# A hybrid RWKV-7 and attention layer: x, w_o blocks and early up products around the first norm, issued in another order

## The chip, the cores and the metric

The kernel runs on one core of one Trainium2 chip. The metric is the device time of one execution in microseconds (us); the number that is compared is the median of several executions. All times below are of this kernel on this one core. TensorE runs at 1.2 or 2.4 GHz; the profile gives the granted clock of a stretch as a share of the higher level, so that 0.50 is the lower one.

## What is computed

One step of a single layer for 512 new frames (`x_prompt`) and 128 further frames of running streams (`x_sample`), 2048 columns wide, all in float32. Half of the columns go through an RWKV-7 recurrence, half through an attention with forget gates; both meet in `w_o`, and a norm and an MLP with another norm follow. The change concerns the lines from `w_o` to `w_up`:

```python
    mix = jnp.concatenate([y_r, y_f], axis=-1) @ w_o
    h = layer_norm(ALPHA * x + mix, ln1_g, ln1_b)
    ffn = jnp.square(jax.nn.relu(h @ w_up)) @ w_down
    out = layer_norm(ALPHA * h + ffn, ln2_g, ln2_b)
```

## The kernel before

**Tiles.** The 640 frames are five token tiles (t = 0 to 3 from `x_prompt`, t = 4 from `x_sample`) of 128 rows. Every float32 product is made of three TensorE matmuls on a high and a low part of each side (`three`). A raw tile is split into them by two instructions: ScalarE copies it to the high part, and VectorE subtracts that from the raw tile for the low part.

**w_o.** The 2048 output columns are four groups n of 512. For groups 1 and 2 a loop takes eight steps s; each loads a block of 256 rows of `w_o` (`rawo{n}_{s}`, 0.52 MB), splits it (`hio`, `loo`) and adds 5 x 2 x 3 = 30 matmuls into five PSUM banks `po{n}_{t}` (`tokens`). `OB = (1, 4, 4)` gives raw blocks one buffer, high and low parts four each. When a group ends, `add_x` fetches a piece of x (`xz`, 128 x 512, 0.26 MB) for each token tile, adds it to the bank (into `acc[t]`) and takes its statistics, and the bank is free for the next group. `xz` has two buffers, and the first holder of one is `gbr`, the norm's gain and offset, read later by a transpose. The adds of group 0 (whose products stand earlier) run in the middle of group 1. Group 3 is done for each token tile apart (`last_columns`), with the tile's norm and its store to `hscr[t]`.

**The up products.** The MLP's first product is a Strassen-like scheme on halves of 320 tokens and 1024 rows: the normed tile h, transposed, gives blocks `11` and `21` (made by `first_tokens`: transposes on TensorE, gain and offset and high part on ScalarE, low part on VectorE) and `22`, `t1` to `t4` (made by `sums(k)`, k = 0 to 7: four groups of transposes into banks b12, b22, b11, b21, then about a dozen vector steps). A loop over pairs of column blocks (`pair(i)`, seven products of 24 matmuls each) uses them all; the raw weights of a pair, `rw`, are loaded by `load_w` into the tiles that held `acc`. To have TensorE at work while the sums are made, the products of the first four pairs with `11` and `21` are taken ahead: `early(i, j)`, 24 matmuls each into a bank `pe{i}`, j = 0 with block `11`, j = 1 with `21`. Their weights are two quarters (`we`), each loaded, split (`hie`, `loe`) and used. After j = 0 ScalarE copies the bank to `xe`, after j = 1 it applies the ReLU.

**Buffers.** The tag `s` of the pool `stgu` is a ring of four: raw tiles of `first_tokens`, the raw quarters of the early weights, and two tiles for each call of `sums` (`t0_k`, `t1_k` in the trace: b12s and t1, t2 and b22s) take their turn in it. High parts of early weights have three buffers, low parts two. PSUM is split in five banks `pq` and three `pd`.

**Order.** TensorE's order is that of the program text (`manual_schedule` for that engine); the orders of VectorE, ScalarE, GpSimd and of SyncE, which issues the loads and stores, are set by the scheduler of the framework. An engine works its instructions off in order: one that waits holds all behind it, on SyncE too.

Of the kernel before, what the change touches and what calls it, by code (L numbers as in the profile page):

```python
# [11 lines left out]
F32 = mybir.dt.float32  # L12
F32R = mybir.dt.float32r
BF16 = mybir.dt.bfloat16
AF = mybir.ActivationFunctionType
# [4 lines left out]
P = 128  # L20
# [149 lines left out]
def hybrid_layer_kernel(  # L170
# [1001 lines left out]

    lst = [lnp.tile([P, 4, 6], F32, name=f"lst{t}", bufs=1) for t in range(NTT)]

    def add_x(n, t, pt):

        a = acc[t][:, n * 512:(n + 1) * 512]
        xz = lnp.tile([P, 512], F32, tag="xz", name=f"xz{n}{t}", bufs=2)
        SY.dma_start(xz, xrows(t)[:, n * 512:(n + 1) * 512])
        V.scalar_tensor_tensor(out=a, in0=xz, scalar=ALPHA, in1=pt, op0=ALU.mult, op1=ALU.add)  # L1180
        V.bn_stats(out=lst[t][:, n, :], in_=a)

# [19 lines left out]
    for n in range(1, 3):  # L1202
        pts = [bank(f"po{n}_{t}") for t in range(NTT)]
        for s in range(8):
            tokens(w_o, s * 256, 2, n * 512, yT.hi, yT.lo, 2 * s, pts,
                   s == 0, s == 7, f"o{n}_{s}", b=OB)
            if n == 1 and s == 4:
                for t in range(NTT):
                    add_x(0, t, acc[t][:, 0:512])
        for t in range(NTT):  # L1210
            add_x(n, t, pts[t])
# [3 lines left out]

    pts = [bank(f"po3_{t}") for t in range(NTT)]
    for s in range(4):
        tokens(w_o, s * 256, 2, 1536, yT.hi, yT.lo, 2 * s, pts, s == 0, False, f"o3_{s}", b=OB)
    ends = [split([w_o[s * 256:s * 256 + 256, 1536:2048].rearrange("(k p) f -> p k f", p=P)], [P, 2, 512], f"o3_{s}", OB)
            for s in range(4, 8)]  # L1220

    def last_columns(t):
        for s, (hi, lo) in enumerate(ends):
# [56 lines left out]
    def early_weights(i, j):  # L1280

        ws = []
        for q in range(2):
            w = quarter(f"we{i}{j}{q}")
            r0 = (8 * j + 4 * q) * P
            SY.dma_start(w, w_up[r0:r0 + 4 * P, 2 * i * P:2 * i * P + P].rearrange("(k p) f -> p k f", p=P))
            ws.append(parts_w(w, f"e{i}{j}{q}"))
        return ws

    for t in range(4):  # L1290
        last_columns(t)
    parts("11", ((c11p, "c11h"), (c11p, "c11l")))
    first_tokens("11", 0, range(KH))
    first_weights = early_weights(0, 0)
    last_columns(4)
    ln.close()

# [14 lines left out]
    def sums(k):  # L1312


        b12 = turn_h(bank(f"b12_{k}"), k, True)
        b22 = turn_h(bank(f"b22_{k}"), KH + k, True)
        b11 = turn_h(bank(f"b11_{k}"), k, False)
        b21 = turn_h(bank(f"b21_{k}"), KH + k, False)
        two = [stgu.tile([P, 2, HF], F32, tag="s", name=f"t{n}_{k}", bufs=4) for n in range(2)]
        b12s, t1, t2, b22s = two[0][:, 0, :], two[0][:, 1, :], two[1][:, 0, :], two[1][:, 1, :]  # L1320
        t3, t4 = b22s, b12s

        def out(b, raw, shift=None):
            oh, ol = (x[:, k, :] for x in H[b])
            if shift is None:
                A.activation(oh, raw, AF.Copy)
                V.tensor_tensor(out=ol, in0=raw, in1=oh.bitcast(F32), op=ALU.subtract)
            else:
                A.activation(oh, raw, AF.Identity, bias=shift)
                V.scalar_tensor_tensor(out=ol, in0=raw, scalar=shift, in1=oh.bitcast(F32), op0=ALU.add, op1=ALU.subtract)  # L1330

        A.activation(b12s, b12, AF.Copy, scale=gain(k))
        A.activation(b22s, b22, AF.Copy, scale=gain(KH + k))
        V.scalar_tensor_tensor(out=t1, in0=b11, scalar=minus[:, 0, k:k + 1], in1=b12s, op0=ALU.mult, op1=ALU.add)
        V.tensor_tensor(out=t2, in0=b22s, in1=t1, op=ALU.subtract)
        out("t2", t2, offset(KH + k))
        out("t1", t1)
        out("22", b22s, offset(KH + k))
        V.tensor_tensor(out=t3, in0=b22s, in1=b12s, op=ALU.subtract)
        V.scalar_tensor_tensor(out=t4, in0=b21, scalar=gain(KH + k), in1=t2, op0=ALU.mult, op1=ALU.subtract)  # L1340
        out("t3", t3, minus[:, 1, k:k + 1])
        out("t4", t4)
# [24 lines left out]
    xe = stgu.tile([P, 5, HF], F32, tag="o", name="xe")  # L1367
    banks = []

    def early(i, j, ws=None):  # L1370
        ws = ws or early_weights(i, j)
        if j == 0:
            banks.append((dbank if i < 3 else bank)(f"pe{i}"))
        product(banks[i], None, ("11", "21")[j], j == 0, f"e{i}{j}", ws)
        if j == 0:
            A.activation(xe[:, i, :], banks[i][:, :HF], AF.Copy)
        else:
            o = xe[:, EARLY, :]
            first_block(o, banks[i])
            SY.dma_start(ascr[2 * i][:, 0:HF], o)  # L1380

    early(0, 0, first_weights)
    first_tokens("21", KH, range(KH // 2))
    early(1, 0)
    first_tokens("21", KH, range(KH // 2, KH))
    early(2, 0)
    early(3, 0)
    sums(0)
    early(0, 1)
    sums(1)  # L1390
    sums(2)
    early(1, 1)
    sums(3)
    sums(4)
    early(2, 1)
    sums(5)
    sums(6)
    early(3, 1)
    sums(7)

    def load_w(i):
        rw = []
# [101 lines left out]
        V.tensor_tensor(out=lo, in0=ahead[6], in1=hi.bitcast(F32), op=ALU.subtract)  # L1504
        first_w.append((hi, lo))

    rw = load_w(0)
    for i in range(LAST + 1):
        here, rw = rw, load_w(i + 1) if i < LAST else None
        if i == LAST:  # L1510
# [129 lines left out]
```

## Time and profile before

| | |
|---|---|
| median of three runs | 3416.46 us (3408.83 to 3418.71) |
| the profiled execution | 3415.92 us, its span 3414.1 us, mean granted clock 0.978 |
| TensorE busy | 3252.2 us (95% of the span) |
| VectorE busy | 1972.6 us (58%) |
| ScalarE busy | 1200.5 us (35%) |
| GpSimd busy | 474.4 us (14%) |

Times of the trace count from the span's start. How its views read: a *window* gives a stretch, its length, the busy us of TensorE (PE), its weight load (PEld), VectorE (DVE), ScalarE (ACT) and GpSimd (POOL), each with its count of instructions, then the granted clock, the busy share of the DMA engines and GB/s. The *waits* of an engine are grouped by what released it. A *timeline* gives start, duration, engine, line, operation, output<-inputs by the program's names without their numbers, and in brackets the idle time before and its releaser; SPq is SyncE issuing a DMA. The *chain* is the work that ended last, followed back from the end. L161 is the matmul of `PE.matmul`, L166 its transpose, both helpers that all stages share, so stages are told apart by tile names.

### The profile page before, as it was taken

Reading aid. Unit: us, or ns where it says so; the run is one execution under the profiler, and the core shown is the slowest. Engines: PE = TensorE matmul, PEld = TensorE weight load, DVE = VectorE, ACT = ScalarE, POOL = GpSimd, SP = SyncE. Lnnn points to the kernel's source line nnn. Section 1 sums busy time; section 2 is a strip of 40 time slices with the busy share of each in tenths; the row PEclk is TensorE's granted clock in tenths of the full one; section 3 lists DMA queues with packets and bytes.
Section 4 is the critical chain, followed back from the end, with each engine's and each line's share of the span. In section 5 each row is a group of like instructions: output and inputs, shape, how many; then the busy total and the mean of one; then the engine's idle time right before and its main releaser. Section 6 shows DMA issues by size and latency. Waiting matters only on the chain.

```text
span 3414.1 us, 54975 instructions
## 1 busy us (share of the span) xinstructions
PE 3252.2 (95%) x20864; PEld 2913.9 (85%) x20864; DVE 1972.6 (58%) x4938; ACT 1200.5 (35%) x2406; POOL 474.4 (14%) x817
## 2 busy tenths in 40 slices
PE   8999999999999998989779999999999999999997
PEld 7988889888888897767579999999987888888886
DVE  4487776666767584323477777777774333332335
ACT  3344444444443444212433343434432212221112
POOL 2233333232333312000000000000000000000003
PEclk9999999999999999999789999999999999999999
DMA  4442334342424345223243323333363223332232
GB/s 135 109 117 63 98 105 108 94 122 78 125 78 127 93 113 157 80 90 114 72 146 101 130 98 126 102 126 102 120 246 105 91 95 105 105 107 78 87 103 83
DMA packets 361595, 369.84 MB, mean 108 GB/s; under 512 B 42814, under 2 KB 280882, under 8 KB 359794
## 3 DMA queue, kind: packets, MB, share of 16 engines
q1 hardware_dynamic: 361186, 365.82, 35.0%
q8 instruction: 164, 2.69, 0.3%
q0 software_dynamic: 144, 0.51, 0.1%
q14 instruction: 101, 0.83, 0.1%
HBM read 303.28 MB, written 63.48 MB: 107 GB/s over the span
## 4 chain that ended last, share of the span: by engine, by line
PE 56%; DMA 3%; DVE 3%; ACT 1%; issue 1%; SPq 0%; POOL 0%; DVEq 0%; ACTq 0%; POOLq 0%
PE pw L161 24%; PE B L161 10%; PE C L161 6%; PE A L161 6%; PE po L161 4%; PE pe L161 1%; DMA rawo<-in_w_o_dram 1%; DMA xz<-in_x_prompt_dram 1%; PE pz L161 1%; DMA we<-in_w_up_dram 0%; PE b L166 0%; DMA gb<-in_ln_g_dram 0%; DMA xz<-in_x_sample_dram 0%; DVE loo L239 0%; ACT hio L238 0%
## 5 line engine op out<-in xcount | busy, mean ns | idle before, releaser
L161 PE MATMUL pw<-hiw,ah 128*128 128x512 f32 x1230 | 484.3, 394 | 1.5 <-DVE acd L1544 1.4
L161 PE MATMUL pw<-low,ah 128*128 128x512 f32 x1230 | 484.0, 393 | 0.1
L161 PE MATMUL pw<-hiw,al 128*128 128x512 f32 x1230 | 483.9, 393 | 0.0
L239 DVE TENSOR_TENSOR low<-raww,hiw 128x1024 fp32r<-128x1024 f32 x123 | 150.6, 1224 | 428.8 <-ACT hiw L238 428.7
L238 ACT ACTIVATE hiw<-raww 128x1024 fp32r<-128x1024 f32 x123 | 130.2, 1059 | 587.6 <-PE pw L161 586.5
L161 PEld LDWEIGHTS pw<-hiw,ah 128*128 128x128 f32 x1230 | 231.5, 188 | 55.5 <-DVE acd L1544 2.8
L161 PEld LDWEIGHTS pw<-hiw,al 128*128 128x128 f32 x1230 | 231.6, 188 | 53.2
L161 PEld LDWEIGHTS pw<-low,ah 128*128 128x128 f32 x1230 | 231.6, 188 | 52.8 <-DVE low L239 0.5
L161 PE MATMUL po<-hio,yh 128*128 128x512 f32 x320 | 134.8, 421 | 18.8 <-DVE acc L1180 12.3
L161 PE MATMUL po<-loo,yh 128*128 128x512 f32 x320 | 129.5, 405 | 0.7 <-DVE loo L239 0.7
L161 PE MATMUL po<-hio,yl 128*128 128x512 f32 x320 | 129.2, 404 | 0.0
L1596 POOL TENSOR_TENSOR mv<-mv,keep 128x1 f32<-128x1 f32 x5 | 7.1, 1414 | 878.5 <-DVE mv L1595 878.5
L1546 DVE TENSOR_TENSOR acd<-acd,pw 128x512 f32<-128x512 f32 x140 | 93.6, 684 | 61.1 <-PE pw L161 61.1
L1364 POOL TENSOR_TENSOR o<-o 128x320 f32<-128x320 f32 x28 | 20.2, 721 | 752.7 <-ACT o L1363 752.7
L239 DVE TENSOR_TENSOR loo<-rawo,hio 128x1024 fp32r<-128x1024 f32 (+1 forms) x40 | 40.4, 1009 | 112.5 <-ACT hio L238 112.5
L161 PEld LDWEIGHTS po<-hio,yh 128*128 128x128 f32 x320 | 62.5, 195 | 37.3 <-DVE acc L1180 15.5
L238 ACT ACTIVATE hio<-rawo 128x1024 fp32r<-128x1024 f32 (+1 forms) x40 | 35.5, 887 | 157.3 <-PE po L161 87.4
L161 PE MATMUL B<-ht2h,hib 128*128 128x320 f32 x256 | 79.8, 312 | 10.0 <-ACT hib L1276 10.0
L161 PE MATMUL B<-ht4h,hif 128*128 128x320 f32 x256 | 79.4, 310 | 2.7 <-DVE o L1441 2.7
L161 PE MATMUL C<-ht1h,loc 128*128 128x320 f32 x256 | 79.0, 309 | 1.2 <-DVE loc L1277 1.2
L161 PE MATMUL B<-ht2h,lob 128*128 128x320 f32 x256 | 79.8, 312 | 0.2 <-DVE lob L1277 0.2
L161 PE MATMUL C<-h22h,log 128*128 128x320 f32 x256 | 79.0, 309 | 0.7 <-DVE log L1277 0.7
(2463 smaller groups left out, 9791.8 us busy)
## 6 DMA issues: line engine op xcount, KB each, us to landing
rw<-in_w_up_dram SPq DMA_DIRECT2D x128, 512.0 KB
raww<-in_w_down_dram SPq DMA_DIRECT2D x123, 512.0 KB
ascr<-o SPq DMA_DIRECT2D x60, 320.0 KB
ra<-ascr SPq DMA_DIRECT2D x58, 320.0 KB
rawo<-in_w_o_dram SPq DMA_DIRECT2D x24, 512.0 KB
fscr<-fe SPq DMA_DIRECT2D x32, 320.0 KB
rawr<-in_w_in_dram SPq DMA_DIRECT2D x32, 256.0 KB
rawk<-in_w_in_dram SPq DMA_DIRECT2D x32, 256.0 KB
```

The lines of the kernel that those rows point to most:

```text
L161: self.pe.matmul(out, lhsT=lhsT, rhs=rhs, start=start, stop=stop, **more)
L238: A.activation(hi, raw, AF.Copy)
L239: V.tensor_tensor(out=lo, in0=raw, in1=hi.bitcast(F32), op=ALU.subtract)
L1364: G.tensor_tensor(out=o, in0=o, in1=o, op=ALU.mult)
L1546: V.tensor_tensor(out=a, in0=a, in1=pts[t], op=ALU.add)
L1596: G.tensor_tensor(out=rs, in0=rs, in1=mhalf[:, 0:1], op=ALU.pow)
```

## The change

1. `fetch_x(n)` loads the five pieces of column group n of x into one tile `xg{n}`, for n = 0 to 2, before the group's adds: `xg0` and `xg1` in steps 0 and 2 of group 1, `xg2` in step 2 of group 2, as written. `xg0` and `xg2` take the home of the high parts of `11`, `xg1` that of the low parts. `xz` is left for group 3.
2. `split_o` puts raw blocks of `w_o` in turn in two places: the buffer `raw` and the tile `o` of `stgu`, which `xe` takes later.
3. `early_weights` only loads; a product's quarters are split one product later, in `ready`, and the next product's are loaded right behind.
4. `t4` is made in its PSUM bank b21 and no longer in the place of b12s.
5. Early products, sums and transposes of `h21` stand in another order; `load_w(0)` stands ahead of the last two early products.

The numbers of instructions of each engine are the same.

```diff
+    def fetch_x(n):
+        xg[n] = c11p.tile([P, NTT, 512], F32, tag=("c11h", "c11l")[n % 2], name=f"xg{n}")
+        for t in range(NTT):
+            SY.dma_start(xg[n][:, t, :], xrows(t)[:, n * 512:(n + 1) * 512])
+
+    def split_o(s, n):
+
+        turn = (s + 8 * n) % 2
+        raw = (stgu if turn else stg).tile([P, 2, 512], F32, tag=("raw", "o")[turn], name=f"rawo{n}_{s}", bufs=1)
...
     def add_x(n, t, pt):
 
         a = acc[t][:, n * 512:(n + 1) * 512]
-        xz = lnp.tile([P, 512], F32, tag="xz", name=f"xz{n}{t}", bufs=2)
-        SY.dma_start(xz, xrows(t)[:, n * 512:(n + 1) * 512])
+        if n < 3:
+            xz = xg[n][:, t, :]
+        else:
+            xz = lnp.tile([P, 512], F32, tag="xz", name=f"xz{n}{t}", bufs=2)
+            SY.dma_start(xz, xrows(t)[:, n * 512:(n + 1) * 512])
...
-                   s == 0, s == 7, f"o{n}_{s}", b=OB)
+                   s == 0, s == 7, f"o{n}_{s}", parts=split_o(s, n))
+            if n == 1 and s == 0:
+                fetch_x(0)
+            if s == 2:
+                fetch_x(n)
...
-            ws.append(parts_w(w, f"e{i}{j}{q}"))
+            ws.append(w)
...
-    first_weights = early_weights(0, 0)
+    early_raw = early_weights(0, 0)
+    early_parts = [parts_w(w, f"e00{q}") for q, w in enumerate(early_raw)]
...
-        t3, t4 = b22s, b12s
+        t3, t4 = b22s, b21
...
+    EORDER = ((0, 0), (1, 0), (2, 0), (3, 0), (0, 1), (1, 1), (2, 1), (3, 1))
+
+    def ready():
+
+        nonlocal early_raw, early_parts
+        i, j = EORDER[len(begun)]
+        begun.append((i, j))
+        if early_parts is None:
+            early_parts = [parts_w(w, f"e{i}{j}{q}") for q, w in enumerate(early_raw)]
+        if len(begun) < len(EORDER):
+            early_raw = early_weights(*EORDER[len(begun)])
...
-    early(0, 0, first_weights)
-    first_tokens("21", KH, range(KH // 2))
-    early(1, 0)
-    first_tokens("21", KH, range(KH // 2, KH))
-    early(2, 0)
-    early(3, 0)
-    sums(0)
-    early(0, 1)
-    sums(1)
-    sums(2)
-    early(1, 1)
-    sums(3)
-    sums(4)
-    early(2, 1)
-    sums(5)
-    sums(6)
-    early(3, 1)
-    sums(7)
...
-    rw = load_w(0)
+    ready()
+    early()
+    first_tokens("21", KH, range(KH // 2))
+    ready()
+    early()
+    first_tokens("21", KH, range(KH // 2, KH))
+    for ks in ((0,), (1, 2), (3, 4), (5, 6), (7,)):
+        ready()
+        for k in ks:
+            sums(k)
+        if ks == (7,):
+            rw = load_w(0)
+        early()
+    ready()
+    early()
```

SyncE's queue at the start of group 1, as built. Before:

```order
L234 DMA rawo0_15_18535<-in_w_o_dram 128x512
L1197 DMA gbr_18609<-in_ln1_g_dram 16x128
L1197 DMA gbr_18609<-in_ln1_b_dram 16x128
L234 DMA rawo1_0_18622<-in_w_o_dram 128x2x512
L1179 DMA xz00_18802<-in_x_prompt_dram 128x512
L1179 DMA xz01_18806<-in_x_prompt_dram 128x512
L234 DMA rawo1_1_18658<-in_w_o_dram 128x2x512
L1179 DMA xz02_18810<-in_x_prompt_dram 128x512
L1179 DMA xz03_18814<-in_x_prompt_dram 128x512
L234 DMA rawo1_2_18694<-in_w_o_dram 128x2x512
```

And after:

```order
L234 DMA rawo0_15_18535<-in_w_o_dram 128x512
L1180 DMA xg0_18658<-in_x_prompt_dram 128x512 x2
L1218 DMA gbr_18609<-in_ln1_g_dram 16x128
L1218 DMA gbr_18609<-in_ln1_b_dram 16x128
L1186 DMA rawo1_0_18622<-in_w_o_dram 128x2x512
L1180 DMA xg0_18658<-in_x_prompt_dram 128x512 x2
L1180 DMA xg0_18658<-in_x_sample_dram 128x512
L1186 DMA rawo1_1_18664<-in_w_o_dram 128x2x512
L1180 DMA xg1_18736<-in_x_prompt_dram 128x512 x4
L1180 DMA xg1_18736<-in_x_sample_dram 128x512
L1200 DMA xz30_19451<-in_x_prompt_dram 128x512
L1186 DMA rawo1_2_18700<-in_w_o_dram 128x2x512
```

All of `xg1` and a first piece for group 3 now stand ahead of block 1_2; `xg2` (five more) follows behind 1_2 and ahead of 1_3, and no x load stands among the blocks 1_4 to 3_4.

VectorE at the end of group 1, with the adds of its five banks. Before:

```order
L239 TENSOR_TENSOR loo2_1_18994<-rawo2_1_18991,hio2_1_18993 128x1024
L1180 SCALAR_TENSOR_TENSOR acc0_18596<-xz10_18930,po1_0_18617 128x512
L239 TENSOR_TENSOR loo2_2_19030<-rawo2_2_19027,hio2_2_19029 128x1024
L1181 BN_STATS lst0_18604<-acc0_18596 128x6
L1180 SCALAR_TENSOR_TENSOR acc1_18597<-xz11_18934,po1_1_18618 128x512
L1181 BN_STATS lst1_18605<-acc1_18597 128x6
L1180 SCALAR_TENSOR_TENSOR acc2_18598<-xz12_18938,po1_2_18619 128x512
L1181 BN_STATS lst2_18606<-acc2_18598 128x6
L239 TENSOR_TENSOR loo2_3_19066<-rawo2_3_19063,hio2_3_19065 128x1024
L1180 SCALAR_TENSOR_TENSOR acc3_18599<-xz13_18942,po1_3_18620 128x512
```

And after:

```order
L1190 TENSOR_TENSOR loo2_1_18986<-rawo2_1_18983,hio2_1_18985 128x1024
L1190 TENSOR_TENSOR loo2_2_19022<-rawo2_2_19019,hio2_2_19021 128x1024
L1201 SCALAR_TENSOR_TENSOR acc0_18596<-xg1_18736,po1_0_18617 128x512
L1201 SCALAR_TENSOR_TENSOR acc1_18597<-xg1_18736,po1_1_18618 128x512
L1202 BN_STATS lst0_18604<-acc0_18596 128x6
L1202 BN_STATS lst1_18605<-acc1_18597 128x6
L1201 SCALAR_TENSOR_TENSOR acc2_18598<-xg1_18736,po1_2_18619 128x512
L1201 SCALAR_TENSOR_TENSOR acc3_18599<-xg1_18736,po1_3_18620 128x512
L1202 BN_STATS lst2_18606<-acc2_18598 128x6
L1202 BN_STATS lst3_18607<-acc3_18599 128x6
L1201 SCALAR_TENSOR_TENSOR acc4_18600<-xg1_18736,po1_4_18621 128x512
```

The split of block 2_2 has moved ahead of all five adds, and no split stands between the adds.

SyncE's queue from the stores of the normed tiles to the weights of the fourth early product. Before:

```order
L1286 DMA we000_19649<-in_w_up_dram 128x4x128
L1286 DMA we001_19655<-in_w_up_dram 128x4x128
L1230 DMA hscr3_274<-acc3_18599 128x2048
L1230 DMA hscr4_275<-acc4_18600 128x2048
L1286 DMA we100_19775<-in_w_up_dram 128x4x128
L1286 DMA we101_19781<-in_w_up_dram 128x4x128
L1286 DMA we200_19843<-in_w_up_dram 128x4x128
L1286 DMA we201_19849<-in_w_up_dram 128x4x128
```

And after:

```order
L1310 DMA we000_19637<-in_w_up_dram 128x4x128
L1310 DMA we001_19639<-in_w_up_dram 128x4x128
L1254 DMA hscr3_274<-acc3_18599 128x2048
L1310 DMA we100_19707<-in_w_up_dram 128x4x128
L1310 DMA we101_19709<-in_w_up_dram 128x4x128
L1254 DMA hscr4_275<-acc4_18600 128x2048
L1310 DMA we200_19775<-in_w_up_dram 128x4x128
L1310 DMA we201_19777<-in_w_up_dram 128x4x128
```

The weights of the second product (`we1`) now go out ahead of the last store, those of the third right behind it.

VectorE at sums 1 and 2 (`t0_1` is b12s and t1 of sum 1, `t1_1` t2 and b22s; `ht1l` to `ht4l` are the low parts of the blocks). Before:

```order
L1339 TENSOR_TENSOR t1_1_20009<-t1_1_20009,t0_1_20008 128x320
L1327 TENSOR_TENSOR ht1l_19708<-t0_1_20008,ht1h_19707 128x320
L1335 TENSOR_TENSOR t1_2_20043<-t1_2_20043,t0_2_20042 128x320
L1340 SCALAR_TENSOR_TENSOR t0_1_20008<-b21_1_20004,gbc_18592,t1_1_20009 128x320
L1330 SCALAR_TENSOR_TENSOR ht2l_19710<-t1_1_20009,gbc_18592,ht2h_19709 128x320
L1327 TENSOR_TENSOR ht1l_19708<-t0_2_20042,ht1h_19707 128x320
L1330 SCALAR_TENSOR_TENSOR h22l_19706<-t1_2_20043,gbc_18592,h22h_19705 128x320
L1330 SCALAR_TENSOR_TENSOR ht3l_19712<-t1_1_20009,minus_19715,ht3h_19711 128x320
L1330 SCALAR_TENSOR_TENSOR ht2l_19710<-t1_2_20043,gbc_18592,ht2h_19709 128x320
L1327 TENSOR_TENSOR ht4l_19714<-t0_1_20008,ht4h_19713 128x320
L1339 TENSOR_TENSOR t1_2_20043<-t1_2_20043,t0_2_20042 128x320
L1340 SCALAR_TENSOR_TENSOR t0_2_20042<-b21_2_20038,gbc_18592,t1_2_20043 128x320
```

And after, sum 2 and the start of sum 3:

```order
L1359 SCALAR_TENSOR_TENSOR t0_2_19969<-b11_2_19961,minus_19703,t0_2_19969 128x320
L1360 TENSOR_TENSOR t1_2_19970<-t1_2_19970,t0_2_19969 128x320
L1352 TENSOR_TENSOR ht1l_19696<-t0_2_19969,ht1h_19695 128x320
L1365 SCALAR_TENSOR_TENSOR b21_2_19965<-b21_2_19965,gbc_18592,t1_2_19970 128x320
L1355 SCALAR_TENSOR_TENSOR h22l_19694<-t1_2_19970,gbc_18592,h22h_19693 128x320
L1355 SCALAR_TENSOR_TENSOR ht2l_19698<-t1_2_19970,gbc_18592,ht2h_19697 128x320
L1364 TENSOR_TENSOR t1_2_19970<-t1_2_19970,t0_2_19969 128x320
L1352 TENSOR_TENSOR ht4l_19702<-b21_2_19965,ht4h_19701 128x320
L1301 TENSOR_TENSOR loe010_20014<-we010_19915,hie010_20013 128x512
L1355 SCALAR_TENSOR_TENSOR ht3l_19700<-t1_2_19970,minus_19703,ht3h_19699 128x320
L1301 TENSOR_TENSOR loe011_20018<-we011_19917,hie011_20017 128x512
L1359 SCALAR_TENSOR_TENSOR t0_3_20041<-b11_3_20033,minus_19703,t0_3_20041 128x320
```

Before, the steps of two sums stand mixed; now one sum's stand together, with the split of the next early weights (`loe`) ahead of every second sum's end.

## Rows read from the trace of the kernel before

**Rows 1.** Windows: stretch, length, busy of five engines, granted clock, DMA share, GB/s.

```profile
1493.50:1513.60 20.10, 10.98 (x26) 7.42 (x27) 8.38 (x11) 2.32 (x3) 0.00 (x0) 0.66 0.39 130
1513.60:1558.00 44.40, 44.40 (x192) 36.00 (x191) 8.85 (x8) 7.21 (x7) 0.00 (x0) 1.00 0.22 72
1558.00:1572.00 14.00, 10.84 (x45) 7.97 (x44) 7.07 (x11) 1.15 (x2) 0.00 (x0) 1.00 0.51 169
1626.70:1739.60 112.90, 70.01 (x327) 58.30 (x326) 54.77 (x112) 50.67 (x102) 3.80 (x7) 0.74 0.29 89
1727.00:1739.60 12.60, 4.11 (x14) 3.44 (x14) 6.85 (x13) 3.05 (x6) 0.00 (x0) 0.59 0.97 317
1800.00:1900.00 100.00, 99.32 (x678) 99.09 (x677) 73.94 (x123) 39.67 (x69) 2.16 (x3) 1.00 0.34 110
```

**Rows 2.** Waits of TensorE, 1420 to 1760: releaser, us in total, times, longest.

```profile
PE pe L161 <- ACT hie L1276: 29.6, 6, 7.2
PE po L161 <- DVE acc L1180: 12.3, 6, 5.2
```

**Rows 3.** Timeline of VectorE: start us, duration us, instruction, idle before and releaser.

```profile
1496.17 1.23 DVE L239 TENSOR_TENSOR loo<-rawo,hio 128x1024 fp32r<-128x1024 f32 x1 [4.47 <-ACT hio L238]
1497.92 0.67 DVE L1180 SCALAR_TENSOR_TENSOR acc<-xz,po 128x512 f32<-128x512 f32 x1
...
1667.68 0.48 DVE L1327 TENSOR_TENSOR ht4l<-t,ht4h 128x320 fp32r<-128x320 f32 x1
```

**Rows 4.** Timeline of TensorE.

```profile
1498.64 0.79 PE L161 MATMUL po<-hio,yh 128*128 128x512 f32 x1 [5.16 <-DVE acc L1180]
...
1626.72 0.41 PE L161 MATMUL pe<-h11h,hie 128*128 128x320 f32 x1
...
1634.44 2.29 PE L166 MATMUL h<-keep,acc 128*128 128x128 f32 x12
...
1640.87 0.64 PE L161 MATMUL pe<-h11h,hie 128*128 128x320 f32 x1 [4.13 <-ACT hie L1276]
```

**Rows 5.** Timeline of SyncE's queue: the first load of `gbr`.

```profile
1426.51 0.33 SPq L1197 DMA_DIRECT2D gbr<-in_ln_g_dram  x1
```

**Rows 6.** The chain in order of time: start us, duration us, engine or transfer.

```profile
1422.14 0.62 PE obs L161 x18
...
1432.60 2.56 DMA xz<-in_x_prompt_dram
...
1634.66 5.50 DMA we<-in_w_up_dram
...
1671.35 3.51 PE b L166 x21
...
1682.57 6.20 PE pe L161 x24
...
1739.62 1.74 PE B L161 x10
1741.36 3.52 PE C L161 x24
```

**Rows 7.** Timeline of ScalarE.

```profile
1458.18 1.06 ACT L238 ACTIVATE hio<-rawo 128x1024 fp32r<-128x1024 f32 x1 [4.96 <-DMA rawo<-in_w_o_dram]
...
1640.18 0.63 ACT L1276 ACTIVATE hie<-we 128x512 fp32r<-128x512 f32 x1 [1.36 <-DMA we<-in_w_up_dram]
...
1647.44 0.44 ACT L1376 ACTIVATE xe<-pe 128x320 f32<-128x320 f32 x1 [5.83 <-PE pe L161]
...
1651.63 0.46 ACT L1266 ACTIVATE h21h<-h21r 128x320 fp32r<-128x320 f32 x1
...
1661.66 0.53 ACT L1332 ACTIVATE t<-b,gbc 128x320 f32<-128x320 f32 x1
...
1723.81 0.53 ACT L1332 ACTIVATE t<-b,gbc 128x320 f32<-128x320 f32 x1
1727.32 0.56 ACT L1329 ACTIVATE ht3h<-t,minus 128x320 fp32r<-128x320 f32 x1 [0.71 <-DVE t L1339]
```

## What I expect of the change, and why

> **What bounds the kernel now.** I read the span by stages first [rows 1]. In the pair loop (1800 to 1900) TensorE is busy 99.32 of 100 us; an edit there could only help by taking matmuls away, and this one takes none. The stretch around the norm is different. From 1493.5 to 1513.6 TensorE issues 26 matmuls in 20.10 us, from 1513.6 to 1558 it issues 192 in 44.40, or 0.231 us each; and from 1626.7 to 1739.6, where the early products and the sums of blocks stand, it is busy 70.0 of 112.9 us at a granted clock of 0.74. So I asked what TensorE waited for [rows 2]: 29.6 us for the high parts of the early weights (`hie`) and 12.3 us for `acc`, the add of x. These are what the change works on.
>
> The time is set by TensorE's stalls here and by its work behind them. A microsecond taken out between 1430 and 1740 comes off the end, since the loop behind has no slack to lose it in.
>
> **A. The x loads.** The five adds that end a column group free TensorE's banks, and before, each waits for an x tile that comes through two buffers, one of them first held by `gbr`. At the end of group 1 the second add runs only at 1497.92: VectorE's order has the split of w_o block 2_2 in front of it, and that waited 4.47 us for its high part, so for its transfer [rows 3]. TensorE stood 5.16 us there, and the first matmul behind it took 0.79 us at a clock of 0.66 [rows 4, 1]. Cost: 20.10 us for 26 matmuls, whose work is 26 x 0.231 = 6.0, so 14.1 lost. At the end of group 2 the same sum gives 14.00 - 45 x 0.231 = 3.6 [rows 1]. Together 17.7.
>
> After, the fifteen tiles of groups 0 to 2 are fetched in three pieces before the fourth w_o block of group 1. VectorE's order has block 2_2's split in front of all five adds, and the next split needs buffers that TensorE frees only as the group ends. An add takes 0.67 us [rows 3] and I take its statistics at the same; a bank's last six matmuls 1.4 us of TensorE, so the adds keep pace. I take 17.0 of the 17.7, with bounds 14 and 17.7 (a last wait with half speed behind it, or none).
>
> What x pushes back: SyncE's queue is in order. The first two x pieces stand ahead of `gbr` and the first w_o block and wait for the last `obs` product of the sample attention, done at 1422.76; `gbr` waits, as before, for the last product of group 0 and went out at 1426.51 [rows 5, 6]. The two go out in the 3.7 us between, in which the queue was idle: cost 0. Were that wait to end later, two issues of 0.33 us and 0.52 MB at 317 GB/s would stand ahead of the first block: 2.3 us, the upper bound; the lower is 0, since `gbr` keeps its wait. Behind it 3.93 MB (three w_o blocks of 0.52, nine x pieces of 0.26) have to land before step 2 of group 1. At the 317 GB/s of the stretch to 1739.6 [rows 1] that is 12.4 us, and a lone piece needs 2.56 [rows 6], 1.7 more than its bytes: landed by about 1441.5, split by 1444. Group 1 ends at 1493.5 and a step is 30 x 0.231 = 6.9, so step 2 starts near 1450. Block 1_3, behind five more pieces, lands near 1447 for 1457. Six to seven microseconds of cover, then. Those five pieces also wait for the adds of group 0, and blocks 1_3 onward stand behind that wait; it ends when the first five pieces have landed, by 1433.
>
> **Raw blocks in two places.** A block's turn is 1.06 + 4.96 = 6.0 us [rows 7], a step of TensorE 6.9: the second place removes a wait that cost TensorE nothing. Value 0; the four high and low buffers are the cover. The tile of `xe` and the homes of `h11`, which raw blocks and x now use, are first written after the last block of group 3 is split.
>
> **C. The early products.** From the first early matmul (1626.72) to the first of pair 0 that runs on (1739.62) 112.9 us pass [rows 4, 6]. A round repeats three times: transposes of two sums, vector work until a buffer of the ring `s` is free, transfer and split of the next weights, a product of 6.20 us at half speed; from 1671.35 to 1688.77, 17.4 us [rows 6]. After, weights come a product ahead, so transfer and split leave the round. What is late next is the sums: `s` has four places, two now hold raw weights through the round, and two sums can no longer overlap.
>
> C1, to the first ACT step of sum 0. Product (0,0) and the first transposes of `h21` stay, 1634.44 + 2.29. Weights (1,0) now go out ahead of `hscr4`, and the wait of 4.13 us at 1640.87 goes [rows 4]. Weights (2,0) come behind it instead, and ACT's order has their split in front of the second half of `h21`: landing like the ones that stood there before, at 1634.66 + 5.50 [rows 6], a split of 0.63, then what ACT does from `xe` to the last `h21h`, 1647.44 to 1652.09, 4.65 with one split in it [rows 7], and one more split, 0.6: 1646.0. C1 = 19.3. TensorE is there by then: 1634.44 + 2.29 + 3.52 + 2.29 = 1642.5, or 1645.2 with the product at half speed. Bounds 16 and 22 (that transfer 3 faster, or product and transposes both 3 late).
>
> C2, from sum 0 to sum 7. Alone, a sum takes from its first ACT step, 1723.81, to the end of `ht3h`, 1727.88, and then the next may use its buffer: 4.1, with the hops between engines 4.6. Sum 0, with two splits between its steps, takes 1661.66 to 1668.16 on VectorE: 6.5 [rows 7, 3]. In VectorE's order every second sum has such splits, so seven spacings are 4 x 6.5 + 3 x 4.6 = 39.8. Bounds 32.2 and 45.5 (all of one kind). `t4` now stays in its bank until `ht4l`, the last but one step of a sum, and the next sum's last transposes wait for that; their consumer comes late in the sum, so nothing is added.
>
> C3, from sum 7 to pair 0: 1723.81 to 1739.62, 15.8. It is the transfer of `rw`, which waits for sum 7's transposes, with its sums and splits, and stays. Products (2,1) and (3,1), 7.0 to 12.4 us, now lie inside it. Bounds 14.5 and 18.
>
> Sum: 19.3 + 39.8 + 15.8 = 74.9 for 112.9, a gain of 38.0.
>
> **A rule weighed.** An early product took 6.20 us in a round and takes 3.52 in the pair loop [rows 6]: half speed after each wait. By the second row a round's TensorE work is 3.5 + 3.5 = 7.0 and hides under two sums (11.1). The Trainium skill (TensorE: Matmul & The Clock Gate, section "A second HAM failure mode: psum-queue depth-cycling") says that matmul groups which cycle through PSUM banks with short idles between swing between the two clock levels and pay for it in each burst. That speaks against this change, which leaves bank waits in each round; by it a round's work stays near 3.5 + 6.2. As a mechanism of this kernel it is the first rival.
>
> **Total.** The profiled execution took 3415.92 us (span 3414.1), 0.5 below the median of 3416.46. 3415.92 - 17.0 - 38.0 = 3360.9: 3361.
>
> **The rivals.**
> - *Half speed in every round.* Transposes and product, 9.7, plus bank waits fill a round: every sum then costs what sum 0 did, C2 45.5, and C1 2.7 more: +8.4, 3369. For it: the clock fell in every round before. Against: the waits in front of it, up to 7.2 us [rows 2], go.
> - *Better cover.* The splits fall into gaps, C2 32.2: 3353.
> - *The round stays* at 17.4 for two sums, so that the change doesn't do what it says: the low parts have two buffers, so a split waits for an earlier product, and VectorE with it. C2 = 3.5 x 17.4 = 60.9: 3382.
> - *x delays the weights.* If a transfer only starts when the one ahead has landed, nine pieces of 2.56 and three blocks of 3.4 bring block 1_2 at 1461, 1_3 at 1477: 14 and 9 us of waits, 3384. Against: the eight pieces of `rw` moved at 317 GB/s together.
> - *Slower.* The one ring makes the round wholly serial: transposes, two sums, product, splits (two on each engine at 0.63) = 3.5 + 13.0 + 6.2 + 2.5 = 25.2. Then 34.9 to sum 0 as before (to 1661.66), 3.5 x 25.2 = 88.2, and 15.8 + 12.4 bare: 151.3, 38.4 over 112.9; less A, 3437. It decides from (112.9 + 17.0 - 34.9 - 28.2) / 3.5 = 19.1 us a round. Against: in TensorE's order both transposes of a round stand before its product, and five banks serve them.
>
> **How the numbers follow.** Forecast 0.64, half speed 0.17, better cover 0.05, the round stays 0.08, x delays 0.03, slower 0.02, no change at all 0.01. The terms' bounds put the forecast between 17.7 and 16 + 32.2 + 14.5 (3348) and 14 - 2.3 and 22 + 45.5 + 18 (3377). The range 3350 to 3380 holds the first three cases, 0.86, less a little at its ends. 0.3%, 10 us, is about what a measurement of this kernel can tell from no change; all cases but the last two gain more.
>
> **What would show it.** In the profile after: no wait of `po` for `acc`, and group 2's first matmuls at full clock; the first w_o block in as early as before; the first `t` of sum 0 about 19 us after the first early matmul, those of sums 1 to 7 in steps of 4.6 and 6.5, then 15.8 to pair 0 with two products inside. Wrong would be: a wait of `po` for `hio` in steps 1 to 3, sums 8 us apart, or a longer gap before pair 0.

## The result, and the profile after

The changed kernel takes 3358.25 us (median of four, 3355.99 to 3359.09) where the one before takes 3412.64 (four runs as well); the ratio is 0.984, with a 95% interval of 0.983 to 0.986. The prediction was 3361 with a range of 3350 to 3380. The profiled execution took 3359.09 us:

```profile
span 3357.3 us, 54979 instructions
PE 3238.1 (96%) x20864; PEld 2903.9 (86%) x20864; DVE 1971.7 (59%) x4938; ACT 1198.2 (36%) x2406; POOL 475.0 (14%) x817
```

A total hides where time went, so cut both spans at the same four events: the end of the last `obs` product of the sample attention (1422.76 before [rows 6]; after 1419.05 + 0.62 = 1419.67), the first early matmul (1626.72 [rows 4]; 1605.83), the end of pair 0's product B, which is the first matmul of C (1741.20; 1685.32), and the end of the span. The windows between, before first and then after (columns as in [rows 1]):

```profile
1422.70:1626.70 204.00, 183.47 (x752) 143.35 (x752) 60.14 (x83) 45.58 (x59) 2.89 (x5) 0.94 0.33 109
1626.70:1741.20 114.50, 71.58 (x338) 59.88 (x337) 56.37 (x114) 50.95 (x102) 3.80 (x7) 0.75 0.28 88
```

```profile
1419.60:1605.80 186.20, 177.03 (x752) 140.54 (x752) 58.78 (x83) 45.58 (x59) 2.88 (x5) 0.97 0.35 119
1605.80:1685.30 79.50, 65.31 (x337) 54.56 (x337) 56.81 (x114) 49.44 (x102) 4.61 (x7) 0.83 0.40 125
```

| stretch | before | after | gain |
|---|---|---|---|
| start to `obs` | 1422.8 | 1419.7 | 3.1 |
| x stretch: `obs` to first early matmul | 204.0 | 186.2 | 17.8 |
| sums stretch: to the end of pair 0's B | 114.5 | 79.5 | 35.0 |
| the rest | 1672.9 | 1672.0 | 0.9 |
| span | 3414.1 | 3357.3 | 56.8 |

In the sums stretch TensorE's idle time fell from 42.9 to 14.2 us, and its busy time by 6.3, with the same matmuls: fewer ran at the lower clock level (granted 0.75 before, 0.83 after). The waits of TensorE, 1420 to 1700, after (releaser, us in total, times, longest):

```profile
PE po L161 <- ACT hio L1189: 6.6, 1, 6.6
PE b L166 <- DVE ht4l L1352: 6.3, 3, 2.2
PE B L161 <- ACT hib L1300: 3.0, 1, 3.0
PE pe L161 <- DVE loe L1301: 2.3, 1, 2.3
PE pe L161 <- DVE ht4l L1352: 2.1, 1, 2.1
...
```

Both waits of [rows 2] are gone. Of waits of about 2 us and more there are left one for the first w_o block of group 1, four for `ht4l` (a PSUM bank of the sums; 1.9 to 2.2 each), one for a low part of the first early weights, which stood there before as well, and the wait for the first operand of pair 0. That last one was 10.0 before and is 3.0, since products (2,1) and (3,1) now run inside it. Before:

```profile
1735.34 0.64 PE L161 MATMUL B<-ht2h,hib 128*128 128x320 f32 x1 [10.01 <-ACT hib L1276]
```

ScalarE's first step of each sum (L1357 into `t`) shows the pace of the sums after the change:

```profile
1624.68 0.53 ACT L1357 ACTIVATE t<-b,gbc 128x320 f32<-128x320 f32 x1
...
1631.33 0.51 ACT L1357 ACTIVATE t<-b,gbc 128x320 f32<-128x320 f32 x1
...
1635.84 0.51 ACT L1357 ACTIVATE t<-b,gbc 128x320 f32<-128x320 f32 x1
...
1643.71 0.52 ACT L1357 ACTIVATE t<-b,gbc 128x320 f32<-128x320 f32 x1
...
1647.64 0.51 ACT L1357 ACTIVATE t<-b,gbc 128x320 f32<-128x320 f32 x1
...
1655.60 0.53 ACT L1357 ACTIVATE t<-b,gbc 128x320 f32<-128x320 f32 x1
1660.58 0.51 ACT L1357 ACTIVATE t<-b,gbc 128x320 f32<-128x320 f32 x1
...
1667.08 0.53 ACT L1357 ACTIVATE t<-b,gbc 128x320 f32<-128x320 f32 x1
```

Sum 0 starts 18.85 us after the first early matmul; then come spacings of 6.65, 4.51, 7.87, 3.93, 7.96, 4.98 and 6.50, together 42.4; then 18.24 from sum 7 to the end of B.

### The profile page after: what moved, and what is told of

The parts are those of the page before. It is cut to its first block, busy times and chain, and to the rows that moved or that the text cites. A ratio compares the mean times of both kernels' runs of the same rounds, so it can differ in the third digit from the quotient of the medians.

```text
span 3357.3 us, 54979 instructions
## 1 busy us (share of the span) xinstructions
PE 3238.1 (96%) x20864; PEld 2903.9 (86%) x20864; DVE 1971.7 (59%) x4938; ACT 1198.2 (36%) x2406; POOL 475.0 (14%) x817
## 4 chain that ended last, share of the span: by engine, by line
PE 58%; DVE 2%; DMA 2%; issue 1%; ACT 1%; SPq 0%; DVEq 0%; POOL 0%; ACTq 0%
PE pw L161 24%; PE B L161 10%; PE C L161 7%; PE po L161 6%; PE A L161 6%; PE pz L161 1%; PE pe L161 1%; DMA gb<-in_ln_g_dram 0%; DMA yt<-yscr 0%; DVE acd L1637 0%; DVE acd L1564 0%; PE h L166 0%; PE ob L161 0%; PE sc L161 0%; PE pbfv L161 0%
## 5 line engine op out<-in xcount | busy, mean ns | idle before, releaser
L1190 DVE TENSOR_TENSOR loo<-rawo,hio 128x1024 fp32r<-128x1024 f32 x24 | 29.4, 1224 | 100.3 <-ACT hio L1189 100.2
L161 PE MATMUL B<-ht2l,hib 128*128 128x320 f32 x256 | 79.9, 312 | 0.0
```

What stands on the lines that cost most here:

```text
L161: self.pe.matmul(out, lhsT=lhsT, rhs=rhs, start=start, stop=stop, **more)
L1190: V.tensor_tensor(out=lo, in0=raw, in1=hi.bitcast(F32), op=ALU.subtract)
```

## The experiments

In each run the two stretches are read from its trace as above, since they repeat better than the total. How well, the runs say themselves: over the nine that have the x part as changed, the x stretch lies between 185.5 and 187.4 us, and over the five that have the early part as changed, the sums stretch lies between 78.1 and 80.4. Each is read from one execution, so a difference of 2 us between two runs tells nothing; these two ranges are the spread that is meant below.

**Does it add up?** Run e1 has the x part alone, run e2 all but the x part.

> The kernel before with only the x part of the change (x fetched a column group ahead, raw w_o blocks in two places); early products and sums as before. Theory: the x part and the early part add up, so this alone shortens the stretch from the last product of the sample attention (obs) to the first early matmul by 17.8 us, as in the changed kernel's trace (203.96 to 186.16), and leaves the stretch from there to the end of pair 0's B at 114.6: 3395 against 3412.6, gain 15 to 20. Rival: the early part before has slack that takes the time up again (weights of the first products not in time when the norm comes earlier); then the second stretch grows and the gain is under 10 us: over 3403.

> The changed kernel without its x part: x through two buffers and w_o blocks through one as before, early products, sums, t4 and load_w as changed. Theory (parts add up): first early matmul as late as before, then 79.5 us to the end of pair 0's B in place of 114.6, gain 33 to 37 against before: 3376 to 3380. TensorE waits for acc again for 12 us. Rival (the early part needs the x part): more than 84 us in that stretch, above 3383.

Measured: e1 3390.79 us, ratio 0.994 (0.992 to 0.995); e2 3372.87, ratio 0.988 (0.987 to 0.990). The stretches of e1, then of e2:

```profile
1422.10:1608.40 186.30, 177.04 (x754) 140.81 (x753) 58.82 (x83) 45.62 (x59) 2.88 (x5) 0.97 0.35 119
1608.40:1720.70 112.30, 69.17 (x338) 57.47 (x338) 56.38 (x114) 51.01 (x102) 3.81 (x7) 0.74 0.29 90
```

```profile
1421.30:1626.20 204.90, 183.34 (x752) 142.95 (x753) 60.13 (x83) 45.57 (x59) 2.88 (x5) 0.94 0.33 108
1626.20:1705.40 79.20, 64.72 (x338) 53.40 (x338) 55.97 (x114) 48.92 (x102) 4.54 (x7) 0.85 0.40 125
```

Each part shortens its own stretch by what it does in the whole (17.7 of 17.8, 35.3 of 35.0) and leaves the other within 2.2. They add up, and in e2 TensorE waits for `acc` again (13.4 us). The totals came out lower than expected, by 4 us for e1 and 3 under the range for e2; against the kernel before on the same chip (3410.50) they gain 19.7 and 37.6.

**What in the sums stretch does it?** The prediction said: weights come a product ahead. Run e3 takes that lead away and keeps the place of `ready()` ahead of a round's sums:

```diff
-            early_parts = [parts_w(w, f"e{i}{j}{q}") for q, w in enumerate(early_raw)]
-        if len(begun) < len(EORDER):
-            early_raw = early_weights(*EORDER[len(begun)])
+            early_parts = [parts_w(w, f"e{i}{j}{q}") for q, w in enumerate(early_weights(i, j))]
```

> The changed kernel, but an early product's weights are loaded and split in its own round (at ready) and no longer a product ahead; the new order of products and sums stays. Theory of the prediction (the gain is that transfer and split leave the round): a transfer of 2.9 us, two splits of 0.63 and 0.69 and the half speed behind the wait come back in each of the four rounds with sums, 5 to 6 us each: the stretch to the end of pair 0's B grows from 79.5 to about 100 and the time to 3378. Rival (the new order alone does most of it, since the product now stands behind the transposes of both sums and its weights come in while VectorE works on them): at most 88, under 3367.

Measured: 3360.9, ratio 0.985 (0.984 to 0.987), stretch 83.7. The theory falls: without the lead, 30.8 of the 35.0 us are still there, and both numbers are the rival's. Run e5 then also moves the place, with no lead:

```diff
-        ready()
         for k in ks:
             sums(k)
         if ks == (7,):
             rw = load_w(0)
+        ready()
         early()
```

> The changed kernel, but a round's weights are loaded and split only after the transposes and steps of its sums in program order (ready stands behind the sums, and loads for its own product), as in the kernel before; the order of TensorE's work stays the changed one. Theory (place of the load): what took the transfer and the splits out of the round is that they are asked for ahead of the round's sums, since the ring of four gives places in program order; behind them the transfer waits for the sums' tiles again, TensorE waits for hie 4 to 7 us in every round and the rounds take 14 to 17 us: the stretch from the first early matmul to the end of pair 0's B is 102 to 112 in place of 83.7 (loaded ahead of the sums, but not a product ahead), the time 3378 to 3390. Rival (order of TensorE's work: product behind both sums' transposes, products and h21 transposes interleaved): the stretch stays under 92, the time under 3369.

Measured: 3382.54, ratio 0.993 (0.991 to 0.994), stretch 103.0. TensorE's waits for the early weights, in e3 and then in e5:

```profile
PE pe L161 <- ACT hie L1300: 9.8, 4, 4.5
```

```profile
PE pe L161 <- ACT hie L1300: 29.9, 7, 4.9
```

As much as the 29.6 us of [rows 2] is back in e5. With no lead, then, the place of the load in the program is worth 19.3 us (103.0 - 83.7): a tile asked for behind the sums gets its place in the ring of four only when their vector steps free one. SyncE's waits in front of the early loads show it, first in e5, then in the changed kernel:

```profile
SPq L1310 <- DVE t L1360: 43.8, 4, 15.2
```

```profile
SPq L1310 <- DVE loe L1301: 25.6, 7, 12.1
```

With the place ahead, the lead of a product is worth 4.2 (83.7 - 79.5), and not in the rounds: in e3 sum 0 starts 5.8 us later, but the sums run 5.8 closer, so sum 7 starts 61.25 us into the stretch in both. What e3 loses lies behind that, where the last product waits 4.5 us for weights that stand behind the loads of `rw`. What e5 keeps of the change (order of products and `h21`, `t4`, `load_w`) is 11.5 (114.5 - 103.0), and it lies ahead of the sums: sum 0 starts 22.7 us into the stretch, not 34.9. The order alone, which was e3's rival, is thus not the reason either. The other way round, run e6 has the lead, but `ready()` behind the sums:

> The changed kernel with the splits of a product's weights, and the loads of the next, behind the round's sums in program order (ready stands behind the sums); the loads are still a product ahead. Theory (place of the load): raw weights are in a whole round early, so only the splits (0.63 + 0.69) and the half speed behind them can show; in exchange no split stands ahead of a sum's steps on ScalarE, so the sums run 1 to 3 us closer: stretch 77 to 82 in place of 79.5, 3356 to 3362. Rival (splits have to be ahead as well): over 88, 3367 or more.

Measured: 3358.57, ratio 0.986 (0.984 to 0.987), stretch 79.7, as the theory said. The sums do run closer (sum 7 starts at 56.4 us of the stretch, not at 61.2), and one new wait gives it back: the last product's weights stand behind the loads of `rw`.

```profile
PE pe L161 <- ACT hie L1300: 8.7, 1, 8.7
```

So with `ready()` behind the sums the lead is worth 23.3 (103.0 - 79.7), and neither edit alone can be called the one that decides: each does nearly all of it, and only with both gone does the wait return. One condition covers all four runs: a product's weights have to be requested ahead of its own round's sums. In e3 they are by their place, in e6 by the lead (they are asked for at the end of the round before), in the changed kernel by both, in e5 by neither.

**The bank that holds `t4`.** Run e4 undoes one line (`t3, t4 = b22s, b12s`).

> The changed kernel with t4 again in the place of b12s and not in its PSUM bank. The prediction put the cost of the bank being held at nothing; the changed kernel's trace shows 8.4 us of waits of TensorE for ht4l, three in front of transposes and one in front of a product. Theory 1 (the bank held costs): the bank comes free when b21 is read, four VectorE steps of 0.45 earlier, the four waits shrink by 1.8 each and the rounds with them: 3 to 7 us faster, 3351 to 3355. Theory 2 (the ring of four is what sets the pace): the place of b12s is held to the end of the sum instead, so the next tile of the ring comes later, the waits change their name and the time is the same or up to 3 us longer: 3357 to 3361.

Measured: 3357.28, ratio 0.984 (0.983 to 0.986), stretch 80.7: the second theory. The waits for `ht4l` went, and these came in their place:

```profile
PE b L166 <- DVE t L1365: 5.8, 3, 2.2
PE b L166 <- ACT t L1357: 2.8, 3, 1.5
```

With 0.8 in front of a product that is 9.4 us, where the changed kernel's waits in the sums come to 9.0: TensorE waits for the pace of the sums, by whatever name. 80.7 is 0.3 above the spread.

**The second place for raw blocks.** Run e7 sets `turn = 0`.

> The changed kernel with all raw blocks of w_o in the one buffer, as before. The prediction gave the second place the value 0, since a block's turn (6.0 us) is shorter than TensorE's step (6.9): 3358 within 2 us, no wait of po for hio behind the first block of group 1. Rival (x pieces stand among the blocks, so the blocks need the lead of a second place): one to three waits of po for hio or loo of 1 to 4 us in group 1 and half speed behind them, 3361 to 3368.

Measured: 3358.44, ratio 0.986 (0.985 to 0.987), `obs` to first early matmul 187.9 where 186.2 and, in a repeat (e9), 186.0 stood; its one wait for `hio` is the first block's. That is 0.5 above the spread. The value is 0 to 2 us, as forecast, below what the total can tell.

**The x pieces ahead of the first block.** Run e10 has `fetch_x(0)` one step later, and e9 is the changed kernel again on the same chip.

> The changed kernel as it is, beside the next three on the same chip. Every theory: 3358 within 3 us, 186 from the last obs product to the first early matmul and 79.5 from there to the end of pair 0's B.

> The changed kernel with x's first group fetched one step later in program order, so that only one piece of x goes out ahead of the norm's gain and the first w_o blocks of group 1, the rest behind block 1_0 and 1_1. With x pieces ahead, 10.4 to 10.7 us passed from the last obs product to the first matmul of group 1; without, 9.6. Theory (the two pieces ahead cost the first block about 1 us): 9.6 to 9.8 here, 1 us faster: 3356 to 3358. Rival (the 1 us is the add of group 0 on VectorE or chance): 10.5 again, same time.

Measured: e9 3360.57, ratio 0.985 (0.984 to 0.987), stretches 186.0 and 80.4; e10 3356.84, ratio 0.985 (0.984 to 0.986), stretches 188.0 and 78.1. The first matmul of group 1 comes 9.7 us after `obs` for 10.6, but the next one waits; first the changed kernel, then e10:

```profile
1430.24 0.79 PE L161 MATMUL po<-hio,yh 128*128 128x512 f32 x1 [6.62 <-ACT hio L1189]
1431.72 0.79 PE L161 MATMUL po<-loo,yh 128*128 128x512 f32 x1 [0.68 <-DVE loo L1190]
```

```profile
1425.25 0.80 PE L161 MATMUL po<-hio,yh 128*128 128x512 f32 x1 [5.72 <-ACT hio L1189]
1428.53 0.79 PE L161 MATMUL po<-loo,yh 128*128 128x512 f32 x1 [2.48 <-DVE loo L1190]
```

In the ten runs with two pieces ahead, group 1's first matmul comes 10.2 to 11.2 us after `obs`. But e12 below has the same edit as e10 and has it at 10.7, so that the 1 us was theirs is not shown. It is no gain in either: the wait moves to the low part (2.5 us here and 2.0 in e12, for 0.7). In the changed kernel's chain x's transfer ends on an add of group 0 that stands ahead of this split on VectorE; that the later x holds the split in e10 in the same way was not tried apart.

**The end of the stretch.** In the changed kernel, as built, the loads that follow sum 7 go out with two of pair 1's (`rw1_1`) in front of pair 0's, since sum 7's transposes free the tile of `acc3` first. Run e8 turns the tiles by one (`tag=f"acc{(2 * i + q + 3) % 4}"`, and with it the home of two tiles that are loaded at the end of the pair loop).

> The changed kernel with the tiles of rw turned by one, so that pair 0's first weights go to the tile of acc3, which the transposes of sum 7 free first, and no longer behind two loads for pair 1 (1.05 MB, 3 us at 350 GB/s). Theory (the end of the stretch waits for rw's transfer): 11.7 us from sum 7's first ScalarE step to pair 0's first matmul become 8 to 10 and the stretch 2 to 3 us shorter: 3355 to 3357. Rival (what is late there is the last sum's ht3h, held on ScalarE behind the copy that waits for the store of the one ascr tile, and the second half of the weights): no change, 3358.

Measured: 3352.21, ratio 0.984 (0.982 to 0.985), stretch 75.9, 2.2 under the shortest of the five, with TensorE's wait for pair 0's first operand 0.7 in place of 3.0 and B's end 3.6 us sooner; the total, 3 us under the range of the theory, doesn't tell it from the changed kernel's (0.984 too). That the transfer alone does it is not shown, since VectorE's order changed with the tiles. Pair 0's weights are first read by `sa`; in the changed kernel it stands behind `ht3l`, which waits for `ht3h`, in e8 ahead of it:

```profile
1676.11 0.66 DVE L1355 SCALAR_TENSOR_TENSOR ht3l<-t,minus,ht3h 128x320 fp32r<-128x320 f32 x1 [2.34 <-ACT ht3h L1354]
1676.69 0.68 DVE L1450 TENSOR_TENSOR sa<-rw 128x512 f32<-128x512 f32 x1
```

```profile
1672.98 0.69 DVE L1450 TENSOR_TENSOR sa<-rw 128x512 f32<-128x512 f32 x1
...
1675.77 0.66 DVE L1355 SCALAR_TENSOR_TENSOR ht3l<-t,minus,ht3h 128x320 fp32r<-128x320 f32 x1 [1.10 <-ACT ht3h L1354]
```

In the kernel before, `sa` did wait for the transfer, until 9.4 us after sum 7's first step; in the changed one it runs 9.6 after it, behind `ht3l`, so there the two may have ended at about the same time. The kernel before:

```profile
1733.21 0.69 DVE L1428 TENSOR_TENSOR sa<-rw 128x512 f32<-128x512 f32 x1 [3.98 <-DMA rw<-in_w_up_dram]
```

So the rival's wait is on the path of the changed kernel too. In e8 it stands as before (3.7 us, 3.6 in the changed kernel), but pair 0's first weights no longer stand behind it. It is the store of the ReLU result:

```profile
ACT xe L1388 <- DMA ascr<-xe: 4.1, 2, 3.7
ACT hib L1300 <- DVE sb L1451: 2.1, 1, 2.1
```

Run e11 gives that result (of product (2,1)) its own tile, which pair 0's results then also use:

> The changed kernel with rw's tiles turned by one (as in the run before) and the third of the four ReLU results in a tile of its own, so that ScalarE doesn't wait for the store of the one before (3.66 us at the end of the sums, in front of the last ht3h). Theory (with rw early, that wait is next): pair 0 starts 1 to 2 us earlier, the stretch is 74 to 75 for 75.9, the time 1 to 2 us under the turned kernel's: 3350 to 3353. Rival (the second half of rw is next): the wait goes, the stretch stays at 75.5 to 76.

Measured: 3355.25, ratio 0.984 (0.982 to 0.985), stretch 78.8. The wait went, the gain did not come: `ht3h` waits 2.0 for VectorE instead, and pair 0's B takes 7.2 us with a wait of 1.7 for a low part inside it, where e8's takes 5.0. Of the 2.9 us to e8, 1.2 lie ahead of sum 7 (62.6 for 61.4 us into the stretch), in code that the edit leaves alone. The rest is in B: VectorE has the `sa` of the second half of the weights ahead of that low part, and it waits for the transfer:

```profile
1677.33 1.04 DVE L1450 TENSOR_TENSOR sa<-rw 128x512 f32<-128x512 f32 x1 [0.74 <-DMA rw<-in_w_up_dram]
```

That is the wait that the rival named, though the stretch lies outside its range as well. Whether it comes of the edit is open.

**All together.** Run e12 has x later, the turned tiles, the own tile, and `ready()` behind the sums but its last loads ahead of `rw` in the program.

> All that the runs pointed to together: x one step later, the splits behind the round's sums (with the last loads ahead of rw), rw's tiles turned, the third ReLU result in its own tile. Theory (late order on ScalarE was hidden only by the last product's weights, which stood behind rw): sums 5 us closer together, pair 0 begins without the wait of 8.7 for the last product's weights; the stretch is 70 to 73 for 79.5 and the time 7 to 10 us under the changed kernel's: 3348 to 3352. Rival (the waits change their names): the stretch is 75 to 77, the time as the turned kernel's.

Measured: 3353.41, ratio 0.984 (0.982 to 0.985), beside 3360.57 for e9 on the same chip; the intervals overlap. The total is that of the turned kernel, as the rival had it, and just outside the theory's range. Its sums stretch tells more:

```profile
1608.80:1681.30 72.50, 62.79 (x337) 52.47 (x337) 56.58 (x114) 48.30 (x102) 4.39 (x7) 0.86 0.45 139
```

It is 7.0 us shorter than the changed kernel's (7.9 than e9's) and inside the theory's 70 to 73; the x stretch (187.2) is within the spread. A wait of 4.3 for the last product's weights is left: as built, SyncE's queue still has three of the loads of `rw` ahead of their first half and four ahead of their second.

## Why the prediction was right, and where not

**The total.** 3361 was forecast, 3358.25 measured; against the profiled execution of before, 55.0 us were forecast, 56.8 came. That is closer than the terms deserve, by luck: 52.8 came from the two stretches, and 3.1 + 0.9 from work that the change leaves alone.

**A, the x loads: right.** 17.0 forecast, 17.8 measured, by the mechanism named: after group 1's first block no wait of TensorE is left until the early products, and the term's two stalls of 14.1 and 3.6 are gone. The cost of the two x pieces ahead was put at 0 with an upper bound of 2.3; the first matmul of group 1 came 1.0 later (10.6 us after `obs` for 9.6), and e10 and e12 don't settle whether by them.

**Raw blocks: right,** value 0 within 2 us (e7).

**C1: right, C2: a size.** C1 was forecast at 19.3 and came at 18.85, by the steps named: the transfer of weights (2,0) was to land 13.4 us after the first early matmul, and their split ends its wait for it at 13.5:

```profile
1619.34 0.63 ACT L1300 ACTIVATE hie<-we 128x512 fp32r<-128x512 f32 x1 [1.36 <-DMA we<-in_w_up_dram]
```

C2 was forecast at 39.8 and came at 42.4, inside its bounds. Spacings of 6.5 and 4.6 in turn were expected; the two behind sums 2 and 4 came out at 7.87 and 7.96. The chain through the first of them:

```profile
1639.37 0.49 DVE t L1364
...
1639.93 2.84 DMA we<-in_w_up_dram
...
1642.86 0.07 ACT hie L1300
...
1643.39 0.42 ACT xe L1415
1643.81 0.43 ACT t L1357
```

Sum 2's t3 step (L1364) frees a place of the ring, the weights of a later product take it (2.84 us), and their split stands on ScalarE ahead of sum 3's first step. The forecast counted the splits, 1.9 us of extra in every second spacing, but not the wait for the transfer in front of one. The other long spacing has another cause. Sum 5's first step (1655.60) stands on ScalarE behind the ReLU of product (0,1), and that waits for the product's end, which takes 5.8 us at a granted clock of 0.58:

```profile
1655.03 0.44 ACT L1388 ACTIVATE xe<-pe 128x320 f32<-128x320 f32 x1 [0.70 <-PE pe L161]
```

**C3: right, but its end was set badly.** 15.8 was forecast to "the first of pair 0 that runs on", 1739.62. There B runs on after a wait of 0.2 us in its midst: it had begun at 1735.34, and fourteen of its 24 matmuls were done. From sum 7 to B's first matmul it took 11.5 us before and 11.7 after (1678.81), so the step stays, as forecast. To B's end it takes 17.39 before and 18.24 after, since B itself took 0.65 more, with more of it at the lower level (granted 0.55 over it, 0.69 before); in the repeat e9 it took 5.8, as in the kernel before. Moved to B's end on both sides, the forecast gain is still 38.0, and 35.0 came: 2.6 of the difference is C2, 0.85 is C3, less 0.45 from C1.

**`t4`: nothing added, for another reason.** The prediction said that the waiting transposes have a late consumer. TensorE did wait 8.4 us for `ht4l`, but e4 shows that without it TensorE waits as long elsewhere, and the time is the same.

**The reason for C: right, but one of two.** The step was "weights come a product ahead, so transfer and split leave the round". They did leave it, and e6 shows that the lead is enough for that. It is not needed, though: e3 keeps 30.8 of 35.0 without it, since `ready()` also moved the request ahead of the round's own sums, in a ring that gives places in program order. The prediction gave the lead all and did not price that second edit. The sum was the same either way, since both edits do the same thing to the round.

**The first rival, half speed in each round,** came true in part. The window over product (3,0), that over (0,1) and that over (2,1) and (3,1):

```profile
1635.80:1641.50 5.70, 5.61 (x24) 5.47 (x24) 5.16 (x11) 3.97 (x9) 0.00 (x0) 0.61 0.04 12
1649.00:1654.80 5.80, 5.80 (x25) 5.70 (x24) 4.21 (x9) 2.97 (x7) 0.00 (x0) 0.58 0.02 6
...
1668.50:1675.60 7.10, 7.10 (x49) 7.04 (x48) 4.44 (x10) 3.47 (x9) 0.00 (x0) 1.00 0.98 315
```

The products right behind waits for a bank, (3,0) and (0,1), still run at a granted clock of 0.58 to 0.61; (1,1), behind another such wait, takes 4.9 us; the last two, behind no wait, take 3.5 us each. The Trainium skill (TensorE: Matmul & The Clock Gate, section "A second HAM failure mode: psum-queue depth-cycling") describes such a swing where TensorE idles briefly between groups that cycle through PSUM banks; the trace agrees for these products, whose waits are about 2 us. C2 lies between the forecast's 39.8 and this rival's 45.5, and one slow product is what sum 5 is late by; but TensorE's work does not fill a round, it waits for the sums. The other rivals are ruled out: C2 is far from the 32.2 of better cover, x delays no block (no wait for `hio` after the first block's), and two sums take 11.2 to 12.9 us together, where a round that stays takes 17.4 and a serial one 25.2.

## What to carry to other kernels

Where several users share a ring of buffers that gives places in program order, a request behind the ring's other users waits for them: here 19 to 23 us over the rounds. Put it ahead of those that run before its product; a lead is one way to do that, a place in the same round another, and either was enough. When an edit does two things, undo each alone and both together before one is called the cause. After a stall is removed, look at the order in which the next stage's tiles come free: pair 0's weights stood behind pair 1's, and the run with the tiles turned had a stretch 3.6 us shorter. Cut two traces at the same events before reading a total, and choose events that stand at the same amount of work.

## What the runs showed that was not expected

The end of the last `obs` product, ahead of everything the change touches, lay between 1413.9 us (e9) and 1422.8 (before) in the profiled executions. The changed kernel itself had it at 1419.7 in one and 1413.9 in the other, so a difference of two single executions carries up to 9 us that the edit has no part in. The x stretch repeats within 1.9 us over nine runs and the sums stretch within 2.3 over five. The two executions of the changed kernel alone (186.2 and 186.0, 79.5 and 80.4) make that look smaller than it is.
